# Norms' transposes evicted twice by ScalarE, and Fourier, hyena and filter products in fp32

## The chip, the cores and the metric

One core of one Trainium2 chip runs the program once. The metric is the device time of one execution in microseconds (us), here the median of three. The engines are TensorE (PE in rows; its weight loads PEld), VectorE (DVE), ScalarE (ACT), GpSimd (POOL) and SyncE (SP), which issues most DMAs.

## What is computed

Two blocks follow each other on one sequence of 512 tokens and 1024 channels, all in float32. The first has two layers, with a context of 256 tokens beside the sequence in the first of them. The core of a layer, cut from the reference:

```python
hx = rmsnorm(x, g_pre_mix[i]) * (1.0 + sc1) + sh1
px = hx @ w_in[i]
attn_x = blocked_attention(q, k_all, v_all)               # 8 heads of 64, keys of ctx and x
four_x = fourier_mix(px[..., F0:H0], w_fourier[i])        # 2-D FFT over tokens and 4 groups of 64, then @ w
hy_x = hyena_mix(px[..., H0:], w_hy_conv[i], b_hy_conv[i], hyena_filter(L, *hy_params), hy_bias[i])
mix_x = jnp.concatenate([attn_x, four_x, hy_x], axis=-1) @ w_out[i]
x = x + ga1 * rmsnorm(mix_x, g_post_mix[i])
fx = rmsnorm(x, g_pre_ffn[i]) * (1.0 + sc2) + sh2
x = x + ga2 * rmsnorm(conv_ffn(fx, ...), g_post_ffn[i])   # layer 0 does the same for ctx
```

hyena_mix is a depthwise convolution of three taps, then a long convolution by FFT with a filter that a small network with sines makes from the positions, then a gate. The second block (two kinds of local attention, then a mixture of experts) is not touched by the change.

## The kernel before

TensorE products are made of float32r passes. An operand is split into a rounded part "hi" (ScalarE copies it into a float32r tile) and the rest "lo" (VectorE or GpSimd subtracts); `mm3` (L308 to L312) then runs three passes, hi*hi, hi*lo and lo*hi, into one PSUM bank. `split` (L335 to L338) does both steps. A float32r pass is one TensorE instruction; a plain fp32 product is two.

**Norms.** `to_h` (L477 to L514) scales two token blocks, transposes them on TensorE in 128x128 tiles (L497, PSUM `tps`) and evicts each of the 8 channel blocks of a pair as hi and lo, with a gain and a shift for each channel: ScalarE writes hi (L508), VectorE takes PSUM times gain less hi (L510), and the shift is added by GpSimd for odd blocks (L512) and by VectorE for even ones (L514). `pair` calls it in the feed-forward part and in layer 1's input; layer 0's input calls it directly. There are 11 pairs with a shift, and 88 such evictions. The second block's input has none and goes the other way (L504, L505).

**Filters.** `filters` and `filter` make hyena's filters: layer 0's for x at the very start, the other two beside layer 0's attention. Each block of the filter, `fb`, is split into `kt`, multiplied with the cosine and sine tables `hf` (and their negative `hn`) in `kps`, and summed with alternating signs in `alt`.

**Fourier and hyena.** `fourier` makes W (`wps`), then for each residue r of the tokens `abps` (512 columns, from `Fx` or `Fc`) and `yps` (256 columns, table `tf`), and adds halves up. `hyena` transposes u (`utp`), transforms it (`ups`, table `hf`), multiplies with the filter's spectrum on VectorE and GpSimd (`uva`, `uvb`, `um`, `zs`, `zya`), splits the result into `ys` and transforms back (`iyp`, table `hi`); of the 256 columns of an iyp or yps product often only 128 are used. First x, then, in layer 0, the context.

**Queues and order.** Tables that are split come by `ldr` (L524 to L530) from GpSimd's DMA queue, since their tiles are float32r; weights, fd (Fourier's and hyena's inputs, written out by `mixer_in`), u, x0 and kt come by SP's queue. Work tiles are "pages" of 4 KB a partition: 26 in the main pool, and in layer 1 twelve for Fourier and hyena alone. The framework orders the instructions of each engine by a simulated schedule with the program's order as priority, and adds the semaphores. `gated` adds an edge to that order and no semaphore.

**What stands beside what.** In layer 0, Fourier, hyena and `outA` (the mixer's output product of the attention's half, 12 groups of 12 passes in `dps`, L1508 to L1519) are interleaved by three generators, after the attention. In layer 1, Fourier and hyena are steps beside the attention (`drive`).

Of the kernel before, what the change touches and what calls it, by code (L numbers as in the profile page):

```python
# [14 lines left out]
ALU = mybir.AluOpType  # L15
# [12 lines left out]
def _split(v):  # L28
    v = np.asarray(v, np.float64)
    m, e = np.frexp(v)  # L30
    hi = np.ldexp(np.round(m * 4096.0) / 4096.0, e)
    r = v - hi
    m, e = np.frexp(r)
    lo = np.ldexp(np.round(m * 4096.0) / 4096.0, e)
    return hi.astype(np.float32), lo.astype(np.float32)


# [6 lines left out]
def consts():  # L44
# [17 lines left out]
    hf, hi = (np.stack(_split(np.stack(t, 1))).reshape(2, 128, 1024) for t in (hf, hi))  # L62
    c["hftab"], c["hitab"] = hf, hi
    tf = np.stack(_split(np.stack(tf, 1))).reshape(2, 128, 2, 768)
    c["ftab"] = tf.transpose(0, 2, 1, 3).reshape(4, 128, 768)
# [12 lines left out]
    c["bd64"] = np.stack(_split(bd), 0).transpose(2, 0, 1, 3).reshape(128, 512)  # L78
# [187 lines left out]
class Kern:  # L266
    def __init__(K, tc, A, off, out, dbg=None):
        K.tc, K.nc, K.A, K.off, K.out = tc, tc.nc, A, off, out
        K.dbg = dbg or {}
        K.n = 0  # L270
        K.bal = 0.0
        K.gate = None
        K.marks = []
# [76 lines left out]
    def setup(K):  # L350
# [11 lines left out]
        K.alt = K.cp.tile([128, 4, 4], F32R, name="alt")  # L362
        nc.vector.tensor_copy(K.alt.rearrange("p a b -> p (a b)"), K.sgn[:, 0:16])
# [113 lines left out]
    def to_h(K, xs, tb0, h, cols, dst=None):  # L477
# [14 lines left out]
        for kp in range(4):  # L492
            ps = K.bank([128, 2, 256], name="tps", tag="T")
            for q in range(2):
# [11 lines left out]
                else:  # L506
# [17 lines left out]
    def ldr(K, shape, name, src, pg=None):  # L524

        t = (pg or K.pg)(shape, F32R, name)
        n = int(np.prod(shape[1:]))
        flat = t if len(shape) == 2 else t.rearrange({3: "p a b -> p (a b)", 4: "p a b c -> p (a b c)", 5: "p a b c d -> p (a b c d)"}[len(shape)])
        K.gated(K.nc.gpsimd.dma_start(flat, src))
        return t  # L530
# [61 lines left out]
    def filters(K, later, pg, hf=None):  # L592
# [21 lines left out]
        hf = list(hf or (K.ldr([128, 4, 2, 128], f"hf{p}", A["hftab"][p]) for p in range(2)))  # L614
        hn = pg([128, 2, 4, 1, 128], F32R, "hn")
        for p in range(2):
            nc.scalar.activation(hn[:, p, :, 0], hf[p][:, :, 1].bitcast(F32), AF.Copy, scale=-1.0)
            hf.append(hn[:, p])
# [21 lines left out]
    def filter(K, i, g, h2, w3, dec, hf):  # L640
# [4 lines left out]
        for b in range(nb):  # L645
            p3 = K.bank([128, 512], name="hp3")
            nc.tensor.matmul(p3, h2[:, b * 128:b * 128 + 128], w3, start=True, stop=True, tile_position=(64 * i, 0))
            fb = K.te([128, 2, 256], "hfb")
# [6 lines left out]
            kt = K.wlo([128, 2, 512], F32R, "kt")  # L655
            K.split(kt[:, 0], kt[:, 1], fb.rearrange("p a b -> p (a b)"))
# [4 lines left out]
            kts.append(kt)  # L661
            yield
        alt = K.bank([128, 512], name="alt")[:nb]
        for b, kt in enumerate(kts):
            for z in range(2):
                nc.tensor.matmul(alt, K.alt[:, b, :nb], kt[:, z], start=b == z == 0, stop=(b, z) == (nb - 1, 1))
        ae = K.te([128, 512], "altr")[:nb]
        nc.scalar.activation(ae, alt, AF.Copy)
        yield

        for b in range(nb):
# [5 lines left out]
            for s in range(2):  # L677
                for j, (c, t) in enumerate(((b, s), (rb, 2 * s))):
                    kv = tuple(kts[c][:, z, j * 256:j * 256 + 256] for z in range(2))
                    K.mm3(ps[:, s], tuple(hf[z + 2 if t == 2 else z][:, c * (4 // nb), t % 2] for z in range(2)), kv, j == 0, j == 1)  # L680
# [5 lines left out]
        for q in range(2):  # L686
            for cb in range(2):
                o = (2 * q + cb) * 128
                nc.tensor.transpose(al[:, cb, q, :nb], ae[:, o:o + 128], K.ident[:nb, :nb])
# [48 lines left out]
    def mixer_in(K, i, pair, h, last, mods):  # L738
# [54 lines left out]
        for b in range(2):  # L793
            w = K.wk(K.wload(A["win"][i, 6 + b]), 128)
            for g in gs:
                n = 512 if g == "x" else 256
                ps = K.fm_prod(h, w, g)
                hi, lo = (K.te([128, 512], "fs", F32R)[:, :n] for p in range(2))
                K.split(hi, lo, ps)
                for p, t in enumerate((hi, lo)):  # L800
                    dst = K.fd[p, :, b * 512:b * 512 + 512] if g == "x" else K.fd[2, :, p * 512 + b * 256:p * 512 + b * 256 + 256]
                    nc.sync.dma_start(dst, t.bitcast(F32))
# [327 lines left out]
    def fourier(K, i, out, last, pg, t2):  # L1130

        nc, A = K.nc, K.A
        Fx = [K.ldr([128, 2, 512], f"Fx{p}", K.fd[p], pg) for p in range(2)]
        Fc = None if last else K.ldr([128, 2, 2, 256], "Fc", K.fd[2], pg)
        bd = K.ldr([128, 2, 2, 128], "bd", A["bd64"], pg)
        wf = t2([128, 2, 256], "wf")
        nc.sync.dma_start(wf.rearrange("p a b -> p (a b)"), A["wfour"][i])
        wr = pg([128, 2, 2, 256], F32R, "wr")
        K.split(wr[:, 0], wr[:, 1], wf)
        tf = [[K.ldr([128, 2, 384], f"tf{p}{j}", A["ftab"][2 * p + j], pg) for j in range(2)] for p in range(2)]  # L1140
        W = pg([128, 2, 512], F32R, "Wh"), pg([128, 2, 512], F32R, "Wl")
# [1066 lines left out]
```

## Time and profile before

| | us |
|---|---|
| median of 3 runs | 2352.54 |
| lowest run | 2347.45 |
| the profiled execution | 2355.3 |
| its span, first to last instruction | 2353.5 |

The profiled execution's granted TensorE clock is 0.954 of 2.4 GHz in the mean. In the rows, a line such as `436.73 1.10 PE L1227 MATMUL utp<-ident,x0uc ... x4 [5.31 <-DMA x0uc<-fd]` reads: start, duration, engine, line, operation, output and inputs by the program's names, shapes, count, and in brackets how long the engine had been idle and what ended that. The ends of TensorE's instructions are modelled; the distance of two starts is what tells the pace.

### The profile page before, as it was taken

To read this page: it belongs to the slowest core of one execution; us is meant where nothing else is said; L and a number is where in the kernel's file an instruction comes from. 1 tells how busy PE (TensorE), PEld (TensorE's weight loads), DVE (VectorE), ACT (ScalarE), POOL (GpSimd) and SP (SyncE) were. 2 spreads that over 40 slices of the span, in tenths; PEclk is the share of its full clock that TensorE was granted. 3 is DMA by queue.
4 is the path that set the end of the run, shared out by engine and by line. 5 is a ranking of instruction groups with operands and counts; after the bars stand their busy time and mean duration, and the time that the engine had idled before them with its cause. 6 is when DMAs were issued, how large, how long until landed. Compare 5 with 4: busy or idle time off the path is not lost. (4 is left out here: it accounts for less than half of the span.)

```text
span 2353.5 us, 31469 instructions
## 1 busy us (share of the span) xinstructions
PE 2135.5 (91%) x11958; PEld 1744.1 (74%) x11958; DVE 1522.3 (65%) x2495; ACT 988.6 (42%) x1727; POOL 466.0 (20%) x448
## 2 busy tenths in 40 slices
PE   5899989679999999998987979999989999978895
PEld 2687678568888888886876768888867786756674
DVE  4744675777576777768557465555565645669895
ACT  3533663254322333235443444333344545347672
POOL 1410012221000000014213021000011212126743
PEclk9999999789999999999998989999999999979997
DMA  8363023623322344434130333222233335459993
GB/s 318 102 201 102 10 104 126 227 99 108 121 90 94 122 152 161 157 118 143 59 130 1 134 113 103 94 95 89 99 136 110 82 110 156 164 214 350 319 357 118
DMA packets 96991, 328.85 MB, mean 140 GB/s; under 512 B 11550, under 2 KB 12961, under 8 KB 96836
## 3 DMA queue, kind: packets, MB, share of 16 engines
q1 hardware_dynamic: 80176, 275.39, 33.0%
q0 software_dynamic: 14208, 42.48, 5.7%
q10 hardware_dynamic: 2452, 8.92, 0.9%
q8 instruction: 96, 1.57, 0.3%
q14 instruction: 59, 0.48, 0.1%
HBM read 285.68 MB, written 34.78 MB: 136 GB/s over the span
## 5 line engine op out<-in xcount | busy, mean ns | idle before, releaser
L328 DVE TENSOR_TENSOR wlo<-raw,whi 128x1024 fp32r<-128x1024 f32 x200 | 246.1, 1238 | 174.9 <-ACT whi L327 166.0
L327 ACT ACTIVATE whi<-raw 128x1024 fp32r<-128x1024 f32 x200 | 209.7, 1058 | 266.4 <-PE fps L311 196.6
L310 PE MATMUL fps<-h2x,whi 128*128 128x512 f32 x672 | 262.6, 392 | 4.0 <-DVE cvf L728 4.0
L311 PE MATMUL fps<-h2x,whi 128*128 128x512 f32 x672 | 263.0, 391 | 0.0
L312 PE MATMUL fps<-h2x,wlo 128*128 128x512 f32 x672 | 262.5, 391 | 0.0
L1413 POOL TENSOR_TENSOR cvf<-cvf 128x512 f32<-128x512 f32 x66 | 77.3, 1171 | 762.8 <-DVE cvf L728 681.9
L1336 DVE TENSOR_TENSOR y<-y,dps 128x512 f32<-128x512 f32 x200 | 134.2, 684 | 112.9 <-PE dps L312 112.4
L310 PEld LDWEIGHTS fps<-h2x,whi 128*128 128x128 f32 x672 | 126.5, 189 | 31.4 <-ACT whi L327 4.1
L312 PEld LDWEIGHTS fps<-h2x,wlo 128*128 128x128 f32 x672 | 126.9, 189 | 27.7 <-issue 1.6
L311 PEld LDWEIGHTS fps<-h2x,whi 128*128 128x128 f32 x672 | 127.0, 189 | 26.0 <-issue 0.4
L726 ACT ACTIVATE cvf<-fps,cv 128x512 f32<-128x512 f32 (+1 forms) x126 | 87.5, 695 | 138.6 <-PE fps L312 138.5
L311 PE MATMUL dps<-wlo,actx 128*128 128x512 f32 x352 | 137.1, 389 | 0.0
L310 PE MATMUL dps<-whi,actx 128*128 128x512 f32 x352 | 136.6, 390 | 0.3 <-DVE y L1336 0.3
L312 PE MATMUL dps<-whi,actx 128*128 128x512 f32 x352 | 136.3, 389 | 0.0
L429 DVE SCALAR_TENSOR_TENSOR ma<-wm,cs,ma 128x512 f32<-128x512 f32 x140 | 106.2, 803 | 19.3 <-DMA wm<-in_wmod 19.3
L310 PE MATMUL fps<-hx,whi 128*128 128x512 f32 x288 | 114.0, 396 | 0.5 <-ACT v L949 0.5
L312 PE MATMUL fps<-hx,wlo 128*128 128x512 f32 x288 | 113.3, 394 | 0.0
L311 PE MATMUL fps<-hx,whi 128*128 128x512 f32 x288 | 113.0, 392 | 0.0
L727 DVE SCALAR_TENSOR_TENSOR cvf<-fps,cv,cvf 128x511 f32<-128x511 f32 (+1 forms) x126 | 82.5, 655 | 30.5 <-ACT cvf L726 30.4
L310 PE MATMUL fps<-h2c,whi 128*128 128x256 f32 x336 | 96.3, 287 | 4.1 <-ACT cvf L726 4.1
L311 PE MATMUL fps<-h2c,whi 128*128 128x256 f32 x336 | 96.2, 286 | 0.0
L312 PE MATMUL fps<-h2c,wlo 128*128 128x256 f32 x336 | 96.2, 286 | 0.0
(630 smaller groups left out, 5514.5 us busy)
## 6 DMA issues: line engine op xcount, KB each, us to landing
wm<-in_wmod SPq DMA_DIRECT2D x96, 512.0 KB
raw<-in_wup SPq DMA_DIRECT2D x88, 512.0 KB
raw<-in_win SPq DMA_DIRECT2D x52, 512.0 KB
rawp<-in_wexp SPq DMA_DIRECT2D x48, 512.0 KB
raw<-in_wexp SPq DMA_DIRECT2D x48, 512.0 KB
raw<-in_wdown SPq DMA_DIRECT2D x44, 512.0 KB
raw<-in_wout SPq DMA_DIRECT2D x20, 512.0 KB
xd<-xt SPq DMA_DIRECT2D x20, 512.0 KB
```

The costliest lines, as they stand in the source:

```text
L310: mm(out, st[0], mv[0], start=start, stop=False)
L311: mm(out, st[0], mv[1], start=False, stop=False)
L312: K.lastmm = mm(out, st[1], mv[0], start=False, stop=stop)
L327: nc.scalar.activation(hi, raw, AF.Copy)
L328: (nc.gpsimd if pool else nc.vector).tensor_tensor(lo, raw, hi.bitcast(F32), op=ALU.subtract)
L429: o = nc.vector.scalar_tensor_tensor(a, v, c, a, op0=ALU.mult, op1=ALU.add)
L726: nc.scalar.activation(dst, ps, AF.Identity, scale=w[1], bias=w[3])
L727: nc.vector.scalar_tensor_tensor(dst[:, 1:n], ps[:, 0:n - 1], w[0], dst[:, 1:n], op0=ALU.mult, op1=ALU.add)
L1336: nc.vector.tensor_tensor(y[tb][:, c], y[tb][:, c], pss[hf], op=ALU.add)
L1413: nc.gpsimd.tensor_tensor(t[1], t[0], t[1], op=ALU.mult)
```

## The change

It has four parts.

1. `to_h` evicts each transposed block with a shift twice by ScalarE, once rounded (hi) and once in full into `hlo`, and VectorE takes the difference. GpSimd has no part in it any more.
2. The products of Fourier, hyena and the filters take plain fp32 operands (`mm1`, one matmul instead of three passes). The splits of wf, W, ab, ut, ys, kt and of Fourier's input go; the padding of yps to 256 columns goes where it isn't used, and all of iyp's; `alt` is made in four column groups of the array.
3. The tables are fp32 (`ldf`, SP's queue, one copy) instead of pairs (`ldr`, GpSimd's queue). Fewer pages are taken; bd, wf and hn move to other tiles.
4. `outA` gets an edge of order: the last pass of each group comes after the product that was last before it in the program.

```diff
--- before.py
+++ after.py
+    def mm1(K, out, st, mv, start, stop):
+        K.lastmm = K.nc.tensor.matmul(out, st, mv, start=start, stop=stop)
...
                     nc.scalar.activation(hi, ps[:, q], AF.Identity, scale=Ak, bias=Bk)
                     t = K.sm([128, 256], "hlo", bufs=2)
-                    nc.vector.scalar_tensor_tensor(t, ps[:, q], Ak, hi.bitcast(F32), op0=ALU.mult, op1=ALU.subtract)
-                    if k % 2:
-                        nc.gpsimd.tensor_tensor(lo, t, Bk.to_broadcast([128, 256]), op=ALU.add)
-                    else:
-                        nc.vector.tensor_scalar(lo, t, Bk, None, op0=ALU.add)
+                    nc.scalar.activation(t, ps[:, q], AF.Identity, scale=Ak, bias=Bk)
+                    nc.vector.tensor_tensor(lo, t, hi.bitcast(F32), op=ALU.subtract)
...
-    def ldr(K, shape, name, src, pg=None):
-
-        t = (pg or K.pg)(shape, F32R, name)
...
-        K.gated(K.nc.gpsimd.dma_start(flat, src))
+    def ldf(K, shape, name, src, pg=None):
+
+        t = (pg or K.pg)(shape, F32, name)
+        K.gated(K.nc.sync.dma_start(t if len(shape) == 2 else K.flat(t), src))
         return t
...
-            kt = K.wlo([128, 2, 512], F32R, "kt")
-            K.split(kt[:, 0], kt[:, 1], fb.rearrange("p a b -> p (a b)"))
...
-                    K.mm3(ps[:, s], tuple(hf[z + 2 if t == 2 else z][:, c * (4 // nb), t % 2] for z in range(2)), kv, j == 0, j == 1)
+                    nc.tensor.matmul(ps[:, s], hf[t][:, c * (4 // nb)], kts[c][:, j], start=j == 0, stop=j == 1)
...
-        Fx = [K.ldr([128, 2, 512], f"Fx{p}", K.fd[p], pg) for p in range(2)]
-        Fc = None if last else K.ldr([128, 2, 2, 256], "Fc", K.fd[2], pg)
-        bd = K.ldr([128, 2, 2, 128], "bd", A["bd64"], pg)
...
-        tf = [[K.ldr([128, 2, 384], f"tf{p}{j}", A["ftab"][2 * p + j], pg) for j in range(2)] for p in range(2)]
-        W = pg([128, 2, 512], F32R, "Wh"), pg([128, 2, 512], F32R, "Wl")
+        Fx = K.ldf([128, 2, 512], "Fx", K.fd[0], pg)
+        bd = K.ldf([128, 2, 128], "bd", A["bd64"], lambda s, d, n: t2(s, n))
+        wf = K.ldf([128, 2, 256], "wf", A["wfour"][i], lambda s, d, n: t2(s, n))
+        Fc = None if last else K.ldf([128, 2, 256], "Fc", K.fd[2][:, 0:512], lambda s, d, n: pg([128, 4, 256], d, n)[:, 0:2])
+        tf = [K.ldf([128, 2, 384], f"tf{j}", A["ftab"][j], pg) for j in range(2)]
+        W = pg([128, 2, 512], F32, "W")
...
-                K.split(tl[0][:, r % 2], tl[1][:, r % 2], ps)
-                ab.append((tl[0][:, r % 2], tl[1][:, r % 2]))
+                    K.mm1(ps, (Fx if g == "x" else Fc)[:, b, r:r + nb * 127 + 1:nb], W[:, b], b == 0, b == 1)
+                nc.scalar.activation(tl[:, r % 2], ps, AF.Copy)
+                ab.append(tl[:, r % 2])
...
+                        w = 256 if r % 2 and g == "x" else 128
...
-                            K.mm3(ps[:, j], st, mv, s == 0, s == 1)
+                            K.mm1(ps[:, j, 0:w], ab[r][:, s * 256 + ob * 128:s * 256 + ob * 128 + 128],
+                                  tf[cls // 2][:, cls % 2, c0:c0 + w], s == 0, s == 1)
...
-                K.split(ut[0][:, r], ut[1][:, r], ps)
+                nc.scalar.activation(ut[:, r], ps, AF.Copy)
...
-                        K.mm3(ps[:, s], (hf[0][:, cls, s], hf[1][:, cls, s]), (ut[0][:, r], ut[1][:, r]), True, True)
+                        K.mm1(ps[:, s], hf[:, cls, s], ut[:, r], True, True)
...
-            for r in range(nb):
-                K.split(ys[0][r // 2][:, r % 2], ys[1][r // 2][:, r % 2], Y[r], nc.gpsimd if r % 2 else nc.vector)
...
-                        K.mm3(ps[:, 0:w], st, mv, s == 0, s == 1)
+                        K.mm1(ps[:, 0:128], Y[r][:, s, cb * 128:cb * 128 + 128], hi[:, cls, s], s == 0, s == 1)
...
                                 ps = K.bank([128, 512], name="dps", tag="o")
+                                g = K.lastmm
                                 for k in range(4):
                                     K.mm3(ps, mixA.st(k, tb), (ws[k][0][:, c], ws[k][1][:, c]), k == 0, k == 3)
+                                K.gated(K.lastmm, g)
```

## Rows read from the trace of the kernel before

**Rows 1.** The page, part 1: busy us, share of the span, instructions.
```profile
PE 2135.5 (91%) x11958; PEld 1744.1 (74%) x11958; DVE 1522.3 (65%) x2495; ACT 988.6 (42%) x1727; POOL 466.0 (20%) x448
```

**Rows 2.** Busy us of each engine in five stretches, then granted clock, DMA share, GB/s.
```profile
core 0: us, PE busy (x) PEld busy (x) DVE busy (x) ACT busy (x) POOL busy (x), PEclk, DMA share, GB/s
0.00:58.00 58.00, 33.98 (x228) 16.06 (x228) 27.61 (x58) 19.08 (x34) 8.86 (x16) 0.98 0.84 317
58.00:108.00 50.00, 42.23 (x211) 31.64 (x212) 39.77 (x79) 24.77 (x49) 24.50 (x32) 0.95 0.31 100
...
361.00:453.00 92.00, 73.21 (x393) 64.71 (x390) 63.69 (x130) 28.15 (x54) 19.56 (x16) 0.87 0.52 195
480.00:545.00 65.00, 48.58 (x279) 41.24 (x278) 48.55 (x80) 33.14 (x57) 19.57 (x21) 0.86 0.26 90
...
1179.00:1321.00 142.00, 112.97 (x933) 95.97 (x931) 101.67 (x185) 68.14 (x149) 29.09 (x30) 0.90 0.24 84
```

**Rows 3.** Timeline of TensorE: neighbouring passes of abps (512 columns) and kps (256).
```profile
381.16 0.40 PE L312 MATMUL abps<-Wh,Fx 128*128 128x512 f32 x1
381.40 0.40 PE L310 MATMUL abps<-Wh,Fx 128*128 128x512 f32 x1
...
42.39 0.28 PE L310 MATMUL kps<-kt,hf 128*128 128x256 f32 x1
42.51 0.28 PE L311 MATMUL kps<-kt,hf 128*128 128x256 f32 x1
```

**Rows 4.** Timeline of TensorE: plain fp32 products of other parts.
```profile
43.66 2.80 PE L406 MATMUL mps<-wm,cs 128*32 128x256 f32 x48
...
244.98 0.29 PEld L647 LDWEIGHTS hp<-hw,hh 64*128 64x128 f32 x2 [0.17 <-issue]
244.98 1.12 PE L647 MATMUL hp<-hw,hh 64*128 64x512 f32 x2
...
2047.48 0.96 PE L1894 MATMUL rtp<-wrt,xt 128*128 128x20 f32 x8
```

**Rows 5.** Timeline of the end of layer 0's mixer.
```profile
362.20 0.47 PE L310 MATMUL dps<-whi,mixAx 128*128 128x512 f32 x1 [0.75 <-issue]
...
372.98 0.28 PE L310 MATMUL wps<-wr,bd 128*128 128x256 f32 x1
...
420.07 1.70 DVE L338 TENSOR_TENSOR ys<-zyb,ys 128x512 fp32r<-128x512 f32 x1
...
431.25 0.33 SPq L319 DMA_DIRECT2D raw<-in_wup  x1
431.69 0.43 SPq L1209 DMA_DIRECT2D x0uc<-fd  x1
...
436.73 1.10 PE L1227 MATMUL utp<-ident,x0uc 128*128 128x128 f32 x4 [5.31 <-DMA x0uc<-fd]
...
448.18 0.58 PE L310 MATMUL iyp<-hi,ys 128*128 128x256 f32 x1 [7.16 <-ACT ys L337]
```

**Rows 6.** Timeline of layer 1's attention with Fourier and hyena.
```profile
1210.78 1.14 POOL L529 DMA_DIRECT2D hf<-in_hftab  x2 [25.81 <-PE abps L312]
...
1267.53 0.62 PE L1117 MATMUL po<-ident,rr 128*64 128x128 f32 x4 [4.27 <-DVE pvf L1126]
...
1278.60 0.58 PE L310 MATMUL iyp<-hi,ys 128*128 128x256 f32 x1 [7.66 <-ACT ys L337]
```

**Rows 7.** Instructions of tiles abps and utp: ns min/median/max, first and last start.
```profile
L338 DVE TENSOR_TENSOR ab<-abps,ab x10: 678/686/692, 388.6 to 1211.4; 128x512 fp32r<-128x512 f32 x10
...
L338 DVE TENSOR_TENSOR ut<-utp,ut x10: 414/416/425, 381.2 to 1243.5; 128x256 fp32r<-128x256 f32 x10
```

**Rows 8.** Groups of the norms' evictions (busy, mean ns, idle), and one pair's timeline.
```profile
L508 ACT ACTIVATE h2x<-tps,mc,mc 128x256 fp32r<-128x256 f32 x32 | 16.6, 559 | 27.8 <-PE tps L497 27.8
L510 DVE SCALAR_TENSOR_TENSOR hlo<-tps,mc,h2x 128x256 f32<-128x256 f32 x32 | 14.1, 478 | 15.5 <-ACT h2x L508 15.5
L512 POOL TENSOR_TENSOR h2x<-hlo,mc 128x256 fp32r<-128x256 f32 x16 | 9.8, 614 | 34.2 <-DVE hlo L510 34.2
...
512.04 1.02 ACT L508 ACTIVATE h2x<-tps,mc,mc 128x256 fp32r<-128x256 f32 x2 [1.12 <-PE tps L497]
```

More of the change, by code (lines that the diff above doesn't have):

```diff
@@ L24 @@
 EPS = 1e-6
[L28 to L35, printed above, removed]
 def _linspace(a, b, n):
@@ L61, in consts @@
         tf.append(np.stack([s_, c_, -s_], 1))
[L62 to L65, printed above, removed]
+    c["hftab"], c["hitab"] = (np.stack(t, 1).reshape(128, 1024) for t in (hf, hi))
+    c["ftab"] = np.stack(tf, 1).reshape(128, 2, 768).transpose(1, 0, 2)
     h = np.where(n128 == 0, 0.5, 1.0)
@@ L77, in consts @@
         bd[1, g * 64:g * 64 + 64, g * 64:g * 64 + 64] = -np.sin(a) * sc
-    c["bd64"] = np.stack(_split(bd), 0).transpose(2, 0, 1, 3).reshape(128, 512)
+    c["bd64"] = bd.transpose(1, 0, 2).reshape(128, 256)
     zs, ds = [], []
@@ L271, in __init__ @@
         K.bal = 0.0
-        K.gate = None
+        K.gate = K.lastmm = None
         K.marks = []
@@ L590, in wlo, with filters @@
         return K.wp.tile(shape, dt, tag="wlo", name=name, bufs=K.NW)
-    def filters(K, later, pg, hf=None):
+    def filters(K, later, pg):
         nc, A = K.nc, K.A
@@ L613, in filters @@
             K.gated(nc.sync.dma_start(hx[64:128], K.h2d))
[L614 to L618, printed above, removed]
+        hf = K.ldf([128, 4, 2, 128], "hf", A["hftab"], pg)
+        hn = K.t2([128, 4, 128], "hn")
+        nc.scalar.activation(hn, hf[:, :, 1], AF.Copy, scale=-1.0)
+        hf = [hf[:, :, 0], hf[:, :, 1], hn]
         yield
@@ L660, in filter @@
                 pa = ab
-            kts.append(kt)
+            kts.append(fb)
             yield
-        alt = K.bank([128, 512], name="alt")[:nb]
+        alt = K.bank([128, 512], name="alt")
         for b, kt in enumerate(kts):
[L665 to L668, printed above, removed]
+            nc.tensor.matmul(alt[32 * b:32 * b + 32], K.alt, kt.rearrange("p a b -> p (a b)"), start=True, stop=True, tile_position=(0, 32 * b))
+        ae = K.te([128, 512], "altr")[:32 * nb]
+        nc.scalar.activation(ae, alt[:32 * nb], AF.Copy)
         yield
@@ L688, in filter @@
                 o = (2 * q + cb) * 128
-                nc.tensor.transpose(al[:, cb, q, :nb], ae[:, o:o + 128], K.ident[:nb, :nb])
+                nc.tensor.matmul(al[:, cb, q, :nb], ae[:, o:o + 128], K.ident[:32 * nb, 0:32 * nb:32], start=True, stop=True)
         for cb in range(2):
@@ L797, in mixer_in @@
                 ps = K.fm_prod(h, w, g)
[L798 to L802, printed above, removed]
+                t = K.te([128, 512], "fs")[:, :n]
+                K.ev(t, ps)
+                nc.sync.dma_start(K.fd[0, :, b * 512:b * 512 + 512] if g == "x" else K.fd[2, :, b * 256:b * 256 + 256], t)
                 run(2)
@@ L1144, in fourier @@
             for s in range(2):
-                K.mm3(ps[:, s], (bd[:, 0, s], bd[:, 1, s]), (wr[:, 0, b], wr[:, 1, b]), True, True)
-            ps = ps.rearrange("p a b -> p (a b)")
-            K.split(W[0][:, b], W[1][:, b], ps)
+                K.mm1(ps[:, s], bd[:, s], wf[:, b], True, True)
+            K.ev(W[:, b], ps.rearrange("p a b -> p (a b)"))
         yield
@@ L1203, in hyena @@
         nc, A = K.nc, K.A
-        hf = [K.ldr([128, 4, 2, 128], f"hf{p}", A["hftab"][p], pg) for p in range(2)]
-        hi = [K.ldr([128, 4, 2, 128], f"hi{p}", A["hitab"][p], pg) for p in range(2)]
+        hf, hi = (K.ldf([128, 4, 2, 128], n, A[n + "tab"], pg) for n in ("hf", "hi"))
         for gi, g in enumerate(["x"] if last else ["x", "c"]):
@@ L1222, in hyena @@
                 kt.append(t)
-            ut = [pg([128, 4, 256], F32R, f"ut{z}") for z in range(2)]
+            ut = pg([128, 4, 256], F32, "ut")
             for r in range(nb):
@@ L1266, in hyena @@
                 Y = [t[:, 0], t[:, 1]]
-            ys = [[pg([128, 2, 2, 256], F32R, f"ys{z}{j}") for j in range(nb // 2)] for z in range(2)]
-            for r in range(nb):
-                K.split(ys[0][r // 2][:, r % 2], ys[1][r // 2][:, r % 2], Y[r], nc.gpsimd if r % 2 else nc.vector)
             yield
@@ L1299, in hyena @@
                     for s in range(2):
-                        st = tuple(ys[z][r // 2][:, r % 2, s, cb * 128:cb * 128 + 128] for z in range(2))
-                        w = 128 if (cls == 3 and s == 1) else 256
-                        mv = tuple(hi[z].rearrange("p a b c -> p (a b c)")[:, cls * 256 + s * 128:cls * 256 + s * 128 + w] for z in range(2))
-                        K.mm3(ps[:, 0:w], st, mv, s == 0, s == 1)
+                        K.mm1(ps[:, 0:128], Y[r][:, s, cb * 128:cb * 128 + 128], hi[:, cls, s], s == 0, s == 1)
                     tv = t[:, r:r + nb * 127 + 1:nb]
```

22 lines of the change are left out of this document (7 added, 15 removed).

## The prediction

> **What bounds the kernel now.** I read the page's busy shares first [rows 1]: TensorE is busy 91% of the span, so most of the 2353.5 us are its products and only an edit that shortens stretches where it waits, or the products themselves, can move the end. Next I read the busy time by stretches, to see which those are [rows 2]. The weight-streaming middle of the kernel (the feed-forward parts) is solid TensorE at the full clock, and the change doesn't touch it. The change touches four kinds of stretch, and in all of them TensorE has holes: the end of layer 0's mixer, 361 to 453 us, 19 us idle at a mean granted clock of 0.87; layer 1's attention with Fourier and hyena beside it, 1179 to 1321 us, 29 us idle at 0.90; the norms' pairs, of which 58 to 108 and 480 to 545 us are shown, 8 and 16 us idle; and the start, 0 to 58 us, where DMA moves 317 GB/s at a share of 0.84. The clock, in shares of 2.4 GHz, falls to 1.2 GHz for a while behind a hole, so a hole costs more than its length. Last I read the timeline in the two long stretches, to see what the holes wait for [rows 5, 6].
>
> **The products.** A three-pass float32r product of 256 columns costs 3 x 0.12 = 0.36 us, by the distance of neighbours (42.39 to 42.51), and one of 512 columns 3 x 0.235 = 0.71 us (381.16 to 381.40) [rows 3]. Fp32 products of this size are not in the trace, but smaller relatives are, and each is two TensorE instructions [rows 4]: 48 instructions of 256 columns, four of them at a time in different columns of the array, take 2.80 us, so a pass of 256 takes at most 2.80 / 12 = 0.23 us; a product of 512 columns takes 1.12 us with its first load and its drain; eight instructions of 20 columns take 0.96 us, so a load of 128 fp32 columns alone paces an instruction at 0.12 us. I take 0.44, 0.88 and 0.24 us for 256, 512 and 128 columns. Layer 0 has 4 products in wps, 12 in abps, 24 in yps, 12 in ups and 24 in iyp: 64 x 0.36 + 12 x 0.71 = 31.6 us before. After it, 4 + 12 + 8 have 256 columns, 12 have 512 and 40 have 128 (padding to 256 falls away): 24 x 0.44 + 12 x 0.88 + 40 x 0.24 = 30.7 us. Layer 1 (4, 8, 16, 8, 16): 44 x 0.36 + 8 x 0.71 = 21.5 before and 20 x 0.44 + 8 x 0.88 + 24 x 0.24 = 21.6 after. The filters' 40 products of 256 columns gain 40 x 0.08 = 3.2 us, 1.3 of it in the start. So TensorE's own work stays the same within 3 us; what changes is what stands around it.
>
> The second weight load of the 512-column product lies inside its first pass: two loads are over in 0.29 us while the pair lasts 1.12 [rows 4]. The Trainium skill (TensorE: Matmul & The Clock Gate, Part 3: Packing small matmuls, The mechanism) says that a weight load overlaps with running matmuls only when the row group differs. By that, every fp32 pass here would show its load, and the sum would be that of the fourth rival below; the trace does not agree, since both loads have the same rows.
>
> **What hangs on the products.** Before, each operand was split: a rounded copy on ScalarE, the rest on VectorE. Gone from layer 0's stretch on VectorE: wr and one of two Wl (the other becomes a copy) at the price of ab, 0.69, 6 ab at 0.69, 6 ut at 0.42 [rows 7], and 6 ys, of which VectorE has three, 0.7 to 1.70 us each beside GpSimd's (420.07) [rows 5]: 11 us of VectorE, some 5 of ScalarE and 5 of GpSimd. From layer 1's: 0.69 + 0.69 + 4 x 0.69 + 4 x 0.42 + 2.4 = 8 us of VectorE. VectorE was busy 63.7 of 92 and 101.7 of 142 us [rows 2], so this alone is a gain only where the chain passes through it; it does at ys, before iyp.
>
> **The larger part is pages and order.** Fourier and hyena held tables and operands twice, rounded and rest. In layer 1 their pool has 12 pages; Fx 2, bd, wr, tf 4, W 2 and ab 4 fill it, so GpSimd's load of hf waits 25.8 us for the last abps (1210.78) [rows 6], and hyena's first transform can't start before it lands. Afterwards Fx, tf 2, W, ab 2, hf, hi, u, x0 and kt 2 make 12: all of hyena's loads can be issued some 25 us earlier, at about 1185, and hyena can run beside the attention from there on, instead of starving it at the end, where po waits 4.27 us behind hyena's VectorE work (1267.53) and iyp 7.66 us for ys (1278.60) [rows 6]. In layer 0 hyena's context part is last: its x0uc is issued at 431.69 right behind a weight load of 431.25, its transpose waits 5.31 us for it (436.73), and its iyp waits 7.16 us (448.18) [rows 5]. Nothing is left to fill these holes, because TensorE had run the mixer's output products (dps) from 362.20 to 372.98, ahead of the first Fourier product [rows 5]. The new order edge on the last dps product of each of the 12 groups keeps them behind the Fourier or hyena product that the program has before it, so that some 8 of the groups of 12 x 0.23 = 2.7 us come in hyena's second half. It is an edge in the scheduler's order and no semaphore.
>
> The loads move from GpSimd's queue to SP's, 7 tables and operands in layer 0's mixer and 6 in layer 1's where there were 12 and 11, with half of the bytes. On SP they stand in order with the weights' loads, yd, u, x0 and kt: if one waits for a page, all behind it wait, and the weights of wout are next. GpSimd loses that issuing, and its rotations, adds and butterfly parts come earlier. I cost the queue at nothing in the sum, since half of the pages are gone; if that cover fails, a wait like x0uc's 5.3 us per layer comes back.
>
> Layer 0's stretch, as I take it: the x0uc wait 5.3, half of the 10.8 us in which dps ran ahead, 5.4, and about 3.3 of iyp's 7.16, for the ys before it and the half clock behind it: **-14 us**, bounds 0 (the chain only moves) and -24 (the stretch falls to TensorE's own 73 us less what the half clock added, some 68). Layer 1's: 9 of the 11.9 us of the two waits shown, about 3 for the half clock behind them, and 6 for the stretch 1209 to 1220 in which hyena's page wait and Fourier's chain hold up ScalarE: **-18 us**, bounds -3 and -33 (TensorE's own 113 us less the clock). The filters beside layer 0's attention: TensorE +1.9, VectorE and ScalarE less than before; **0**, bounds -3 and +3. The start: one table of 512 KB less is 1.65 us at 317 GB/s, the products +1.3; **0**.
>
> **The norms.** 88 evictions (128x256) get a second ScalarE pass in place of VectorE's 0.478 and an add, on GpSimd 0.614 or more, on VectorE in every second [rows 8]. VectorE's new subtraction is about 0.42, the price of ut's [rows 7]. ScalarE takes 1.02 us for two evictions and has stood idle 1.12 us before them (512.04) [rows 8]: a period of 2.14 us into which four evictions of about 2.0 just fit. From ScalarE's start to the last part the way was 1.02, then 0.88, then 0.61 and is 2.0, then 0.5: equal. Bounds: -7 (an add of 0.61 off the path in each of 11 pairs) and +18 (the 20 periods of the feed-forward pairs grow to transposes 0.6 + 2.0 + 0.4 = 3.0). I take **+1**, near the fit that the row shows; in the mixer's pairs the period is longer still.
>
> One rule speaks against this edit. VectorE's subtraction reads two SBUF operands, where the old one read PSUM. A split that ran beside GpSimd took 1.70 us where 0.68 is usual [rows 5, 7]. The Trainium skill (GPSIMD Engine Reference, Specifications) says that GpSimd shares its SBUF interfaces with VectorE, with contention for instructions that have two SBUF inputs; the trace agrees. By it the 88 subtractions could take up to 1 us each, but 44 of GpSimd's adds, the work beside them, are gone.
>
> **Sum.** The profiled execution took 2355.3 us (span 2353.5), 2.8 over the runs' median of 2352.5. -14 - 18 + 1 = -31: 2324.3 in its terms and **2321.5** in those of the median.
>
> **Rivals.**
> 1. The freed pages let both stretches shrink to TensorE's work: -24 and -33, 2295.5 us. For it: TensorE's holes there are waits for others' work, and VectorE's new totals, 53 and 94 us, fit. Against it: hyena's arithmetic is a chain.
> 2. The chains stay (order on SP and ScalarE, hyena's VectorE work): only the ys splits and half of the x0uc wait are won, -5 and -4, norms +1: 2344.5 us. For it: GpSimd and VectorE slow each other in 1263 to 1280 anyway.
> 3. ScalarE becomes the bound of the norms, with exps, squares and weight roundings between the evictions: all 88 added passes on the path are 88 x 0.51 = 45 us, 45 - 32 = +13: 2365.5 us, slower than before. It decides from about 63 of the 88 on. Against it: ScalarE was busy 33.1 of 65 and 24.8 of 50 us [rows 2].
> 4. The fp32 loads show: two passes per product at 0.12 more, 76 + 52 + 40 products: +40 us, 2361.5 us.
>
> **How the numbers follow.** Chances: forecast 0.48 (its own range 2308 to 2336), first rival 0.18, second 0.22, third 0.08, fourth 0.04. The range leaves out the last two and the first's lower part, and reaches up to where the second rival gains nothing at all, the profiled 2355.3 less 2.8: 2290 to 2353. About 2% (2305.5, 2399.6) is what a measurement of this kernel can tell from no change: faster 0.20 (most of the first rival, a tail of the forecast), same 0.78, slower 0.02.
>
> **What would show it.** In the changed profile: hf's load in layer 1 at about 1185 and hyena's transposes some 30 us earlier against the attention; x0uc no longer behind wup's loads and dps between hyena's products; fewer clock dips in the two stretches; fp32 products at 0.44 and 0.24 us; the norms' period at 2.1 to 2.3 us. Wrong it would be if the stretches keep their length with the holes elsewhere, if the SP queue stands with a table's load ahead of weights, or if ScalarE is full in the pairs.

## The result, and the profile after

The changed kernel takes 2310.85 us (median; runs from 2309.11 to 2316.26) against 2352.32 before, a ratio of 0.9834 with a 95% interval of 0.9809 to 0.9860: 41.5 us less, 1.7%, inside the range and within the 2% that were called "same", 10.6 us below the predicted 2321.5. The profiled execution took 2312.03 us, its span 2310.1, its mean granted clock 0.961. One of the four runs of the kernel before took 4198.28 us; the ratio leaves it out.

Part 1 of the page after, to hold against [rows 1]:

```profile
PE 2129.8 (92%) x11802; PEld 1723.5 (75%) x11802; DVE 1471.8 (64%) x2409; ACT 1012.8 (44%) x1786; POOL 419.6 (18%) x373
```

TensorE has 5.7 us less to do, VectorE 50.5 and GpSimd 46.4 less, ScalarE 24.2 more. So most of the gain is in waits. To find where, both traces are cut at the same products (107.9 us between the first two rows, the same in both, are left out). The table gives the lengths of the stretches between them; the fourth column is the spread over all kernels of this study whose code in that stretch is the changed one.

| stretch | before | after | same code | difference | forecast |
|---|---|---|---|---|---|
| start to layer 0's last input transpose | 108.1 | 100.5 | 98.2 to 103.0 | -7.6 | 0, and part of +1 |
| layer 0's attention with the filters | 146.7 | 137.4 | 137.1 to 141.0 | -9.3 | 0 |
| first dps to the end of layer 0's mixer | 123.0 | 108.3 | 107.2 to 109.7 | -14.7 | -14 |
| layer 0's feed-forward pairs | 52.3 | 53.7 | 52.3 to 55.0 | +1.4 | part of +1 |
| feed-forward, nothing changed | 534.2 | 533.2 | | -1.0 | 0 |
| layer 1's input | 107.1 | 105.3 | 104.3 to 105.5 | -1.8 | part of +1 |
| layer 1's attention, Fourier, hyena | 141.8 | 130.9 | 127.8 to 131.3 | -10.9 | -18 |
| the rest, layer 1's pairs among it | 1012.6 | 1011.9 | | -0.7 | part of +1 |

The lengths add up to -44.6 us at the last product; the span is 43.4 shorter. One row needs a finer cut. In layer 0's attention the time to the 48th of its 160 score products (`sps`) is 41.9 to 45.9 us in every kernel of this study, whatever its code (the last section says why). From there to the first dps it is 94.9 to 95.4 us with the changed code (97.1 in one, with eight pages): 95.1 in the kernel after, 101.1 before. So some 6 of the 9.3 us are the change's.

Four of these stretches by the windows view of the kernel after (busy us of each engine and instructions, then granted clock, DMA share, GB/s), in the order of the table, the first of them cut at the first input transpose:

```profile
core 0: us, PE busy (x) PEld busy (x) DVE busy (x) ACT busy (x) POOL busy (x), PEclk, DMA share, GB/s
0.00:48.20 48.20, 35.17 (x206) 16.33 (x206) 18.92 (x47) 13.15 (x23) 5.87 (x14) 0.89 0.96 368
48.20:100.50 52.30, 44.93 (x222) 32.63 (x222) 35.89 (x73) 38.49 (x78) 19.01 (x23) 0.90 0.29 93
208.40:345.80 137.40, 123.53 (x1038) 94.33 (x1037) 89.11 (x200) 84.99 (x199) 8.62 (x8) 0.99 0.14 51
345.80:454.10 108.30, 100.71 (x451) 81.96 (x450) 68.13 (x132) 31.50 (x58) 22.01 (x16) 0.97 0.48 182
...
1146.30:1277.20 130.90, 112.32 (x880) 90.09 (x878) 90.62 (x173) 65.08 (x143) 19.55 (x17) 0.91 0.21 69
```

The second to fourth of them in the kernel before:

```profile
53.10:108.10 55.00, 43.43 (x224) 32.19 (x223) 44.77 (x95) 28.42 (x56) 26.31 (x34) 0.94 0.29 94
216.00:362.70 146.70, 129.17 (x1054) 99.14 (x1053) 94.27 (x206) 88.51 (x207) 16.67 (x22) 0.94 0.22 76
362.70:485.70 123.00, 104.96 (x529) 90.92 (x528) 79.89 (x152) 38.12 (x69) 26.20 (x20) 0.90 0.41 156
```

Against [rows 2]: layer 0's mixer is now nearly full of TensorE work (100.7 of 108.3 us, clock 0.97; the longest hole left is 5.03 us ahead of iyp at 386.64, and the trace names nothing that ends it), while layer 1's stretch still has 18.6 us of holes and the same clock, 0.91. The timeline shows why, and how the fp32 products run:

```profile
1150.31 0.43 SPq L516 DMA_DIRECT2D hf<-in_hftab  x1
...
1167.48 2.00 PE L303 MATMUL abps<-W,Fx 128*128 128x512 f32 x4
...
1192.64 0.39 PE L1203 MATMUL utp<-ident,u 128*128 128x128 f32 x2
...
1237.42 0.71 PE L303 MATMUL iyp<-hi,zya 128*128 128x128 f32 x4 [1.34 <-DVE zya L526]
1240.79 1.22 PE L303 MATMUL iyp<-hi,zya 128*128 128x128 f32 x4 [2.65 <-DVE hyt L1274]
```

- hf is issued 4 us after the attention's first product ends (1146.3 us), as forecast. Hyena's first transpose ends 46.6 us after it; before the change it was 50.4. Forecast were some 30 us earlier.
- The four instructions of two 512-column products span 2.00 us with the drain; their starts are 0.429 us apart, those of 256 columns 0.216 and of 128 columns 0.112. A product is two instructions and costs 0.86, 0.43 and 0.22 us; forecast were 0.88, 0.44 and 0.24. No weight load lengthens these distances.
- po's wait of 4.27 us and iyp's of 7.66 [rows 6] have become 0.81 and 3.99 (1.34 + 2.65).

### The profile page after: what moved, and what is told of

Same layout as the page of the kernel before. It is cut to its first block, busy times and chain, and to the rows that moved or that the text cites. A ratio compares the mean times of both kernels' runs of the same rounds, so it can differ in the third digit from the quotient of the medians.

```text
span 2310.1 us, 30938 instructions
## 1 busy us (share of the span) xinstructions
PE 2129.8 (92%) x11802; PEld 1723.5 (75%) x11802; DVE 1471.8 (64%) x2409; ACT 1012.8 (44%) x1786; POOL 419.6 (18%) x373
## 5 line engine op out<-in xcount | busy, mean ns | idle before, releaser
L319 DVE TENSOR_TENSOR wlo<-raw,whi 128x1024 fp32r<-128x1024 f32 x200 | 247.3, 1245 | 175.1 <-ACT whi L318 166.2
L299 PE MATMUL dps<-wlo,actx 128*128 128x512 f32 x352 | 137.1, 389 | 0.0
L421 DVE SCALAR_TENSOR_TENSOR ma<-wm,cs,ma 128x512 f32<-128x512 f32 x140 | 107.2, 810 | 19.5 <-DMA wm<-in_wmod 19.5
```

What stands on the lines that cost most here:

```text
L319: (nc.gpsimd if pool else nc.vector).tensor_tensor(lo, raw, hi.bitcast(F32), op=ALU.subtract)
L421: o = nc.vector.scalar_tensor_tensor(a, v, c, a, op0=ALU.mult, op1=ALU.add)
```

## The experiments

All ratios are to the kernel before, which ran again beside each group of experiments, with medians from 2348.87 to 2350.70 us (2352.32 beside the changed kernel). So a difference of two medians from different groups is uncertain by some 3 us. For orientation: changed kernel 0.9834 (0.9809 to 0.9860). Of the experiments with a part undone or put back, only Fourier and hyena undone and the splits put back there have a whole interval above this one; for the others the lengths of stretches, each from one trace, carry the argument.

### Each part undone

**Norms.** VectorE takes the difference from PSUM again, and the shift is an operation of its own.

```diff
-                    nc.scalar.activation(t, ps[:, q], AF.Identity, scale=Ak, bias=Bk)
-                    nc.vector.tensor_tensor(lo, t, hi.bitcast(F32), op=ALU.subtract)
+                    nc.vector.scalar_tensor_tensor(t, ps[:, q], Ak, hi.bitcast(F32), op0=ALU.mult, op1=ALU.subtract)
+                    if k % 2:
+                        nc.gpsimd.tensor_tensor(lo, t, Bk.to_broadcast([128, 256]), op=ALU.add)
+                    else:
+                        nc.vector.tensor_scalar(lo, t, Bk, None, op0=ALU.add)
```

> The changed kernel with the norms' eviction of before (VectorE from PSUM, the shift by GpSimd or VectorE), all else as changed (2310.9 us). By the forecast the norms' edit is worth nothing (+1 us): about 2310. By the theory drawn from the two traces, VectorE was the bound where the mixer's inputs are made (busy 34.6 of 40.5 us in layer 1), so the edit gave some 2.5 us in layer 0's input and 8.5 in layer 1's: undone, 2320 to 2323, and the loss shows between 1041 and 1141 us with a hole that a VectorE eviction ends.

Measured: 2316.60 us, 0.9874 (0.9849 to 0.9898), 5.8 us over the changed kernel's median. The start of one execution differs from the next by some us, so layer 0's input is compared with that of a kernel which begins it at the same time, the one with 8 pages (further below). Windows of the norms undone, then of the other:

```profile
43.80:102.70 58.90, 45.40 (x223) 33.22 (x222) 44.49 (x89) 29.54 (x59) 25.31 (x34) 0.88 0.33 114
```

```profile
44.00:98.20 54.20, 44.60 (x222) 32.86 (x222) 37.19 (x75) 39.46 (x80) 21.07 (x23) 0.91 0.34 118
```

Undone, the stretch is 4.7 us longer, with VectorE busy 44.5 of 58.9 us against 37.2 of 54.2. In layer 1's input it is 107.2 us against 105.3; the expected 8.5 there was a misreading: products had only changed places across the cut I had used. With the edit layer 1's input takes 104.3 to 105.5 us, without it 106.9 to 107.2 (three kernels). So the edit is worth some 6 us by the medians (9 by the ratios), and these two stretches hold 6.6 of it. Part of it is GpSimd's: in layer 0's input of the kernel before, six VectorE operations ended just behind one of the norms' adds on GpSimd, 0.26 to 0.47 us longer than elsewhere, 2.3 us in all (the last section shows the pattern).

**The order edge.** The line `K.gated(K.lastmm, g)` is taken out.

> The changed kernel without the edge of order on outA's last passes. By the forecast the edge gives 5.4 us in layer 0's mixer (half of the 10.8 us in which the output products ran ahead): about 2316, with the first dozen microseconds of that stretch full of dps passes and a hole of some 5 us or more near its end. Rival, that the earlier loads and the missing splits alone close the holes: 2311. Other rival, that the edge does all of that stretch's gain: 2322 and more.

Measured: 2320.06 us (runs from 2310.44 to 2325.92; the trace is of the longest), 0.9868 (0.9836 to 0.9900). Layer 0's mixer takes 117.4 us instead of 108.3. Its timeline of TensorE near the end of that stretch:

```profile
422.17 1.13 PE L1203 MATMUL utp<-ident,x0uc 128*128 128x128 f32 x4 [8.28 <-DMA x0uc<-fd]
433.02 3.19 PE L303 MATMUL iyp<-hi,zya 128*128 128x128 f32 x14 [6.52 <-DVE zya L1240]
```

The two holes of [rows 5] are back, 14.8 us of waits, with dps passes run off at the stretch's beginning. So the missing splits and the new queue alone do not close these holes. The edge does it in two ways. The products that it holds back fill them, and the load of x0uc comes early. SP's queue, without the edge and then in the changed kernel:

```profile
414.59 0.37 SPq L310 DMA_DIRECT2D raw<-in_wup  x1
415.01 0.88 SPq L1185 DMA_DIRECT2D x0uc<-fd  x1
```

```profile
394.40 0.32 SPq L1185 DMA_DIRECT2D x0uc<-fd  x1
...
413.90 3.10 SPq L310 DMA_DIRECT2D raw<-in_wout  x3
```

With the edge x0uc is issued 7.0 us before its transpose (401.41) and ahead of the wout weights, not behind a load of wup.

**The filters.** The pairs of tables, the split `kt` and three passes return for them alone.

```diff
-        hf = K.ldf([128, 4, 2, 128], "hf", A["hftab"], pg)
+        hf = list(hf or (K.ldr([128, 4, 2, 128], f"hf{p}", A["hftp"][p]) for p in range(2)))
...
+            K.split(kt[:, 0], kt[:, 1], fb.rearrange("p a b -> p (a b)"))
...
-                    nc.tensor.matmul(ps[:, s], hf[t][:, c * (4 // nb)], kts[c][:, j], start=j == 0, stop=j == 1)
+                    K.mm3(ps[:, s], tuple(hf[z + 2 if t == 2 else z][:, c * (4 // nb), t % 2] for z in range(2)), kv, j == 0, j == 1)
```

> The changed kernel with the filters of before (split tables from GpSimd's queue, split kt, three passes), the rest as changed. By the forecast the filters' part is worth 0 in the start and 0 beside layer 0's attention: 2311 within 3. By the theory drawn from the traces it gave some 5 us at the start and 9 beside the attention (346 us for the end of that stretch against 362 before): 2322 to 2326, and the attention's end lies some 14 us later against the span's start. Rival between them: only the start, where one table less is loaded, 1.7 to 5 us: 2313 to 2316.

Measured: 2317.11 us, 0.9870 (0.9848 to 0.9893). Layer 0's attention takes 145.0 us (137.1 to 141.0 with the changed code), 99.4 of it behind the 48th score product (94.9 to 95.4, once 97.1); the start and layer 0's input 104.5 (98.2 to 103.0).

**Fourier and hyena**, with their input, their pairs of tables on GpSimd's queue, their splits and three passes; norms, filters and edge stay changed.

> The changed kernel with Fourier and hyena of before (pairs of tables from GpSimd's queue, splits, three passes) and with Fourier's input split again; norms, filters and the order edge as changed. By the forecast this part gives 14 + 18 us less 5.4 for the edge, 26 to 27: 2336 to 2338. By what the other three parts cost when undone (each 6 to 9 us of the 41) only 15 to 20 are left for it: 2325 to 2331.

Measured: 2345.69 us over ten runs, 0.9979 (0.9967 to 0.9992): all but 5 us of the gain is gone, more than either theory had. The trace is of one of the shorter runs (2339.35). It shows layer 0's mixer at 116.6 us (+8.3), layer 1's stretch at 143.1 (+12.2), and 144.3 in layer 0's attention, whose code is not touched; Fourier's tables are again on GpSimd's queue there, which the run with the queue (below) explains. The four parts undone one by one add up to 56 us, not 41.5, and their prices are not a sum: behind the 48th score product of layer 0's attention the filters undone bring back 4.3 us and Fourier and hyena undone 6.9, where the whole change gave 6.0.

### The edge alone

The same two lines as in the change, in the kernel before.

> The kernel before with nothing but the order edge on outA's last passes. By the forecast's size 5.4 us less than before: 2344 to 2347. By the run with the edge undone (about 8 to 9 us lost) 2340 to 2344. Rival: the edge only pays where the pages and splits are gone, since x0uc's wait for its load and the ys splits stay: within 2 us of before.

Measured: 2344.87 us, 0.9974 (0.9964 to 0.9983). Layer 0's mixer goes from 123.0 to 116.8 us, by 6.2; in the changed kernel the edge is worth 9.1 in that stretch. x0uc is issued 57.9 us behind the first dps here, 69.0 before, and its transpose no longer waits. The edge pays without the freed pages, and in these traces more with the rest of the change.

### Splits, queue and pages in Fourier and hyena

**The splits' work put back**, with the fp32 products and single tables kept. ScalarE writes zeros where the rounded part was, VectorE (or GpSimd) adds the value:

```diff
+    def again(K, t, src, eng=None):
+        K.nc.scalar.activation(t, src, AF.Copy, scale=0.0)
+        (eng or K.nc.vector).tensor_tensor(t, src, t, op=ALU.add)
...
-                nc.scalar.activation(tl[:, r % 2], ps, AF.Copy)
+                K.again(tl[:, r % 2], ps)
...
+            ys = [pg([128, 2, 2, 256], F32, f"ys{j}") for j in range(nb // 2)]
+            for r in range(nb):
+                K.again(ys[r // 2][:, r % 2], Y[r], nc.gpsimd if r % 2 else nc.vector)
```

> The changed kernel with the splits' work put back into Fourier and hyena without the split: Fourier's input, W, ab, ut and (in a tile of its own) ys are written by ScalarE with zeros and filled by an add on VectorE, for every second ys on GpSimd. The values, the fp32 products, the single tables and SP's queue stay as changed. Forecast: splits alone are worth some 3 us at ys in layer 0 and little in layer 1, the larger part is pages and order: 2314 to 2318. Theory from the run with Fourier and hyena undone (about 28 us lost in its trace, VectorE full for 20 us before each hole): the splits are most of it: 2325 to 2336, with iyp waiting 7 to 8 us behind ys in both layers again.

Measured: 2321.11 us (the trace is of the shortest run, 2315.04), 0.9884 (0.9865 to 0.9904), 10 us over the changed kernel, between the two. Layer 0's mixer takes 110.4 us (+2.1), layer 1's stretch 135.6 (+4.7), where the waits of [rows 6] are back:

```profile
1239.52 0.69 PE L1103 MATMUL po<-ident,rr 128*64 128x128 f32 x4 [4.99 <-DVE pvf L1112]
1248.53 1.22 PE L303 MATMUL iyp<-hi,ys 128*128 128x128 f32 x4 [5.75 <-DVE ys L334]
```

**The filters' splits put back** in the same way, in `filter`:

> The changed kernel with the work of the filters' splits put back (each block of the filter is written to kt by ScalarE with zeros and filled by an add on VectorE); the products stay fp32, the table single. Theory: the splits set the filters' gain, so 2315 to 2320, with the end of layer 0's attention 4 to 8 us later against its start. Rival: the gain came from the shorter load of the table at the start and from a half clock that fell otherwise: 2309 to 2313. The forecast had 0 for all of the filters' part.

Measured: 2320.49 us, 0.9877 (0.9858 to 0.9895). Layer 0's attention takes 143.8 us, 98.9 of it behind the 48th score product. Six more operations on ScalarE and six on VectorE (205 and 206 instead of 199 and 200 in the window) cost some 4 us there, nearly as much as undoing the filters' part as a whole.

**The tables on GpSimd's queue**, still single and fp32:

```diff
-        K.gated(K.nc.sync.dma_start(t if len(shape) == 2 else K.flat(t), src))
+        K.gated(K.nc.gpsimd.dma_start(t if len(shape) == 2 else K.flat(t), src))
```

> The changed kernel with its fp32 tables loaded by GpSimd's queue, as before, and not by SP's. The forecast put the move at nothing: 2309 to 2313. Rival, that the tables behind one another on GpSimd hold up its adds and rotations at the heads of the stretches: 2314 to 2320, in 0 to 58 us, at 346 and at 1146 us.

Measured: 2317.81 us, 0.9861 (0.9841 to 0.9881). Layer 0's attention takes 145.0 us, 99.2 of it behind the 48th score product, and its timeline has a cause that neither theory named:

```profile
328.17 0.61 POOL L516 DMA_DIRECT2D Fx<-fd  x1 [3.93 <-PE ptp L1092]
...
329.63 1.86 SPq L310 DMA_DIRECT2D raw<-in_wout  x4
...
337.80 1.06 ACT L318 ACTIVATE whi<-raw 128x1024 fp32r<-128x1024 f32 x1 [4.95 <-DMA raw<-in_wout]
339.96 0.80 PE L1077 MATMUL sps<-khlc,qsc 128*128 128x256 f32 x2 [5.17 <-ACT E L1081]
```

The same place in the changed kernel:

```profile
327.91 1.76 SPq L310 DMA_DIRECT2D raw<-in_wout  x4
329.77 0.44 SPq L516 DMA_DIRECT2D Fx<-fd  x1
...
331.72 1.06 ACT L318 ACTIVATE whi<-raw 128x1024 fp32r<-128x1024 f32 x1 [0.57 <-DMA raw<-in_wout]
```

On one queue the tables stand behind the weights of wout. From the other queue they start 1.5 us before these, the weights land later, ScalarE stands at the rounding of the first one for 4.95 us, and the attention's exponentials (E) stand behind it on ScalarE, so TensorE waits 5.17 us. In layer 1 this kernel's stretch is 134.0 us (+3.1).

**Eight pages instead of twelve** in layer 1 (`bufs=12` to `bufs=8` for the tag fx):

> The changed kernel with 8 pages in place of 12 for Fourier and hyena in layer 1: hyena's u, x0 and kt can be loaded only when Fourier's tiles come free, some 20 us later than in the changed kernel. Forecast (free pages let hyena start earlier, worth most of 18 us): 2320 to 2328. Theory that the steps' order sets hyena's start and the loads are hidden: 2308 to 2313, with the first transpose still 45 to 52 us after the attention's first product.

Measured: 2315.28 us, 0.9854 (0.9838 to 0.9871). The times alone leave the two theories open; the trace does not. Hyena's u is now issued 26.9 us after the attention's first product instead of 8.5, but the stretch takes 130.3 us against 130.9, and hyena's first transpose ends 46.0 us after that product against 46.6. So the pages behind hf and hi give nothing. The load of hf itself comes early with eight pages too; that its delay was hidden, the kernel before shows: its two halves landed at 1214.6 and 1215.9 us, 13.5 us or more ahead of hyena's first transpose (1229.43) and 29.8 ahead of its first reader, ups (1245.70).

### What orders layer 1, and a faster version

**Hyena ahead of Fourier** (in `side`, the two generators change places):

> The changed kernel with hyena's steps ahead of Fourier's beside layer 1's attention; same work, same loads. The forecast had the table loads (pages) set hyena's start. The loads now land some 10 us after the attention begins, but hyena's first transpose came 51 us after it, as before the change (48 us). Theory: the order of the steps in the program sets it, so here the transposes come about 35 us earlier, Fourier's products fill what hyena's VectorE chain leaves open (8 us of holes at 1219 to 1243 and half clock behind them), and the kernel takes 2297 to 2305 us. Rival: the holes come from VectorE and GpSimd work that the attention has to wait for wherever it lies; then they only move: 2309 to 2313.

Measured: 2309.26 us, 0.9834 (0.9809 to 0.9858). The first transpose ends 10.0 us after the attention's first product, 36.6 earlier (the expectation's 51 and 48 us were counted from other cuts), so the steps' order in the program sets them. But the stretch only shrinks from 130.9 to 126.8 us: the hole moves. Windows of this kernel:

```profile
1158.00:1182.00 24.00, 21.95 (x171) 17.11 (x170) 18.09 (x41) 12.27 (x29) 2.00 (x3) 0.97 0.26 95
1182.00:1206.00 24.00, 18.51 (x159) 14.98 (x158) 24.00 (x42) 10.12 (x23) 15.26 (x13) 0.93 0.19 64
```

VectorE is busy for the whole of 24 us, with GpSimd beside it for 15; in the changed kernel it is for 18 us ahead of its holes:

```profile
1219.00:1237.00 18.00, 13.16 (x124) 10.48 (x122) 18.00 (x33) 6.31 (x15) 11.57 (x11) 0.91 0.00 1
```

Not all of that is VectorE's own work: 4.1 of the 24 us and 2.3 of the 18 are waits for GpSimd inside its instructions (the last section; counted as what these took over the shortest of their form). Hyena's arithmetic without GpSimd's share was not tried.

**The same, spread thinner.** Hyena ahead, and in `drive` a step less after every second step of the attention, then after every third:

```diff
-        for _ in main:
-            for _ in range(n):
+        for u, _ in enumerate(main):
+            for _ in range(n - u % 2):
```

> The changed kernel with hyena ahead of Fourier in layer 1 and three of these steps for every two of the attention's where there were four. In the run with hyena ahead alone VectorE was full for 24 us (1182 to 1206) and the holes had moved there. Theory: VectorE bounds hyena's arithmetic beside the attention, so spreading it thinner closes holes: 2299 to 2306. Rival: the same VectorE work waits in one chain in either pace, and the end gets longer as steps are left over: 2308 to 2316.

```diff
-            for _ in range(n - u % 2):
+            for _ in range(n - (u % 3 == 2)):
```

> Hyena ahead of Fourier in layer 1, with 2, 2, 1 of their steps to each step of the attention in turn. With 2, 2 the steps ended some 27 us before the attention (VectorE full at 1182 to 1206), with 2, 1 the attention ended 10 us earlier but the steps that were left then cost that back. Theory: between them the two end together and 4 to 8 us of the 10 are kept: 2301 to 2306. Rival: VectorE's work is the same and is only moved: 2306 to 2311.

Measured: 2306.44 us, 0.9811 (0.9793 to 0.9830), and 2304.46 us, 0.9808 (0.9784 to 0.9833). From the attention's first product to the end of layer 1's output products the changed kernel takes 175.1 us (172.0 to 175.5 with the same code), hyena ahead 170.9, spread by halves 171.9 (the attention ends 12.9 us sooner, the steps that are left over then take 9.7 more than usual), spread by thirds 167.1. In the last one VectorE is full nowhere (19.5 of 21 us at most) and the clock is 0.97:

```profile
1152.70:1275.60 122.90, 108.69 (x881) 86.45 (x879) 87.81 (x170) 64.15 (x141) 20.21 (x17) 0.97 0.18 61
```

In the trace it is the best version, 5 to 8 us ahead of kernels with the changed code in that stretch. The median is 6.4 us below that of the changed kernel; the intervals of the two ratios overlap, so a gain in the whole time is likely, not shown.

## Why the forecast came out as it did

The total held, but as a sum with three wrong terms: two stretches that were taken as about 0 gave 16.9 us in these traces, and one of 18 gave 10.9. That they made up for each other is luck.

- **The products: right.** TensorE's work changed by 5.7 us of 2135, and the prices were right within 0.02 us. The fourth rival (loads exposed) is out: two fp32 instructions whose weight loads address the same rows follow each other in 0.112 us at 128 columns.
- **Layer 0's mixer: right, in size and place.** -14 against -14.7. x0uc's wait does go by an earlier load, as forecast, but the edge moves that load: without it the wait comes back as 8.28 us, and the edge alone ends it in the kernel before. So the terms for x0uc and the edge, 5.3 and 5.4, are one, and it measured 9.1 within the change and 6.2 alone. The rest of the change gives 5.6 in that stretch (117.4 against 123.0), where 3.3 was forecast.
- **Layer 1: the step that failed is "hyena can run beside the attention from there on".** The page wait of hf, 25.8 us [rows 6], was read as what holds hyena up. It was hidden, as hf landed well ahead of its first reader and eight pages lose nothing; the transposes moved by only 4 us because `drive` hands out Fourier's steps first, and with hyena's ahead they move by 36.6. What the stretch did gain, 10.9 us, the runs place at some 5 in the splits and 3 in the tables' queue (each from one trace, where the same code differs by up to 3.5). The remaining 3 no run places. The traces show Fourier's first product 4.8 us after the attention's first, and 8.7 before, where its table bd was the third load on GpSimd's queue and landed at 1186.7, 7.4 us after the attention's first product. Behind what is left stands a bound that the second rival had in part: VectorE, full (with its waits for GpSimd) while hyena's arithmetic and the attention share it. The version spread by thirds agrees: VectorE is full nowhere, and the stretch is 3.8 us shorter than with hyena ahead alone; by times it is not shown.
- **The filters beside layer 0's attention: the term of 0 was mis-sized.** With the code of before the stretch takes 143.5 to 146.7 us, with the changed code 137.1 to 141.0; behind the 48th score product it is 99.5 to 101.1 against 94.9 to 95.4 (once 97.1). I had counted TensorE's work and found it unchanged. The splits lie on ScalarE and VectorE, on which the attention's own chain (maximum, exponential, copies) runs, and 6 of each cost some 4 us. The queue, next, costs as much by itself, and the code of before, which has both, no more than 6: they overlap.
- **The queue: "I cost the queue at nothing" failed to the good side.** The 4 us that the other queue costs beside layer 0's attention come from weights that land late and hold up ScalarE. The prediction named the wait of x0uc as the price; it is in another place, and x0uc's load goes by the edge.
- **The norms: sign wrong, +1 against about -6.** The period was read from a feed-forward pair, where ScalarE has the longest part; even there the traces show no cost: layer 0's pairs take 49.1 to 53.0 us to their last transpose without the edit (three kernels) and 48.1 to 50.9 with it, layer 1's 33.8 and 33.4. In layer 0's input VectorE was the engine with the most to do (44.8 of 55.0 us before, 35.9 of 52.3 after), and the prediction passed over the mixers' inputs with "the period is longer still". Rival 3 is out: ScalarE was busy 38.5 of 52.3 us and TensorE's waits for its evictions there were 1.5 us at most.
- **The rule against the norms' edit.** GpSimd lengthened three of the 88 subtractions, one of them badly (below); the other 85 took 0.42 us, as taken.

At the start 0 was forecast. The first input transpose comes at 52.0 to 53.1 us in the three kernels with the filters of before and at 43.8 to 50.5 in the eleven others: the filters' part gives at least 1.5 us there, and how much more stays open, as kernels with the same code differ by 6.6.

## What to carry to other kernels

When an operation is taken off an engine, price it in each stretch by the engine that is fullest there, also when that engine never ends a long wait on TensorE; counting TensorE's work says nothing on it. Count as VectorE's load what it waits for GpSimd when both work on SBUF tiles side by side. A long wait of a load is worth only what the first reader of its data would gain, so look for what else that reader waits for, the program's order among it. Independent products held back for a known hole were cheap and paid in both kernels here; an edge of order can move loads too, so look at the queue after it. Tables that are not urgent belong on the queue behind the weights that are.

## What the hardware showed that was not expected

- **A VectorE subtraction waits for GpSimd to finish.** Timeline of the kernel after, in layer 1's input:

```profile
1044.18 2.77 POOL L1324 TENSOR_TENSOR y<-y,mod 128x1024 f32<-128x1024 f32 x1 [1.61 <-ACT junk L467]
1044.66 2.58 DVE L503 TENSOR_TENSOR hx<-hlo,hx 128x256 fp32r<-128x256 f32 x1
```

The subtraction of 256 columns, 0.42 us by itself, ends 0.3 us after GpSimd's addition of 1024. This is not a slower rate: VectorE waited for nearly all that was left of the other instruction. Over the whole trace, 80 VectorE operations with two inputs in SBUF (by their tiles' names) and 256, 512 or 1024 columns began while a GpSimd operation of 256 columns or more had at least 0.15 us to run. 69 of them ended 0.28, 0.55 or 1.08 us behind its end, by their columns; of 32 that read PSUM two did. The Trainium skill (GPSIMD Engine Reference, Specifications) has the shared interfaces and contention; the trace agrees, and gives the size, which in the prediction ("up to 1 us each") was too small.

- **The granted clock differs between executions of the same instructions.** Windows of the kernel after and of the one without the edge, whose TensorE instructions are the same and in the same order up to this point:

```profile
212.20:216.20 4.00, 4.00 (x39) 3.30 (x39) 2.59 (x4) 1.89 (x4) 0.00 (x0) 1.00 0.34 95
```

```profile
214.70:218.70 4.00, 4.00 (x21) 3.42 (x20) 2.12 (x4) 1.36 (x3) 0.00 (x0) 0.65 0.34 91
```

Behind the same holes one ran at the full clock and the other partly at the half. It makes 137 to 141 us out of the same attention, nearly all of it ahead of the 48th score product, where the mean granted clock is 0.96 in the first of these kernels and 0.85 in the second. So a difference of 3 us in one stretch of one trace is no evidence unless the part with the clock's fall is cut off.
